# First layer of a diffusion step on one core: first modulation group loaded ahead of x, its copy among the squares, products of constants in TensorE's pauses, first weights converted in parts

## The chip, the cores and the metric

One core of one Trainium2 chip runs the whole program. The metric is device time in microseconds (us) of one execution. TensorE (PE) multiplies, VectorE (DVE), ScalarE (ACT) and GpSimd (POOL) do elementwise work, SyncE (SP) issues most loads. Each engine takes its instructions in a fixed order and waits at the first whose data is missing.

## The reference

Two transformer layers with modulation from a condition vector. Cut to what the change touches, which is the start of layer 0:

```python
def ada_modulation(cond, w_mod, b_mod):
    m = jax.nn.silu(cond) @ w_mod + b_mod
    return jnp.split(m, 6, axis=-1)
...
    sh1_p, sc1_p, ... = ada_modulation(cond_ctx, w_mod[l], b_mod[l])
    sh1_s, sc1_s, ... = ada_modulation(cond_lat, w_mod[l], b_mod[l])
    hp = rms_norm(xp, norm_mix[l]) * (1.0 + sc1_p) + sh1_p    # 128 context tokens
    hs = rms_norm(xs, norm_mix[l]) * (1.0 + sc1_s) + sh1_s    # 512 latent tokens
    p = h @ w_in                                              # both streams, 1024 features in
```

All numbers are float32. Behind it come attention, a feed-forward block and a second layer, which the change does not touch.

## The kernel before

The 640 tokens (512 + 128) lie along the free axis, the 1024 features along the partitions in eight k-tiles of 128. A tile is worked in two halves of 320 tokens (HALF); the second half is split into 192 and 128 where the two streams need different modulation (HCOND), so a step on one k-tile has pieces of 320, 192 and 128 columns.

Float32 accuracy comes from splitting: an operand becomes a rounded high part and a low part, the rest, and a product is three matmuls, high x high, high x low, low x high (mm3). For weights, `unit` loads the raw tile (`load`, into the pool rawp of three buffers), ScalarE copies the high part and VectorE subtracts for the low part. For the activations, Mod.make works on one k-tile and one half: VectorE multiplies x by gain and root (h00t), ScalarE adds the shift and rounds (h00h, the high part), VectorE takes the rest (h00l, the low part).

The stage at the start has these steps, in this order of issue:

- SyncE loads vec, the eight tiles x, and then modulation weights (mraw) and the first three weight tiles (wA0r, wA1r, wA4r).
- Norm.add: ScalarE squares each half of each x (n00sq), VectorE sums them (n00acc). Norm.rstd sums over the partitions by a product with ones on TensorE (n00p); ScalarE takes the logarithm and the exponential of it (n00rs, the root).
- The modulation comes in four groups (mod0, j = 0 to 3), each for two k-tiles. A group's rows are products of the condition (scol) with 2 x 1024 KB of weights, eight instructions for each of two loads; ScalarE copies the result (modsb); two small products with sel turn it into columns, called the turn of the group here; VectorE adds the bias (mods) and makes gains (gs).
- `made(j)` issues the turn of a group and Mod.make of its two k-tiles; `first(ks, us)` issues the weight products of k-tiles ks with weight units us (0, 1 and 2 stand for wA0, wA1 and wA4), twelve matmuls for two halves and two k-tiles in one unit. Their results (wA0a, wA0b, wA1a, wA1b and two banks called wA) collect over all eight k-tiles. Then the products ckv0a begin with the next weights.

The order on TensorE is written out by hand: `run` issues pieces one behind the other, each marked as issued after TensorE's last instruction; `after(inst, fn)` does the same for one instruction of another engine. Where nothing is marked, a scheduler places instructions by its own estimate. The order at the start is:

```python
        nrm.rstd(0)
        run([lambda: nrm.rstd(1)] + rows(0))
        run([lambda: made(0)] + rows(1))
        run([lambda: first((0, 1), [0]), lambda: made(1), lambda: first((0, 1), [1, 2])])
        run(rows(2))
        run([lambda: first((2, 3), [0]), lambda: made(2), lambda: first((2, 3), [1, 2])])
        run(rows(3))
        run([lambda: first((4, 5), [0]), lambda: made(3), lambda: first((4, 5), [1, 2])])
        run([lambda u=u: first((6, 7), [u]) for u in range(3)])
```

## Time and profile before

| what | value |
|---|---|
| median of 3 runs | 1495.97 us (1495.92 to 1497.59) |
| the profiled execution's own time | 1495.85 us |
| its span | 1494.1 us |
| granted TensorE clock, mean | 0.993 |
| TensorE busy | 1445.6 us (97%) |
| VectorE, ScalarE, GpSimd busy | 1210.5, 762.8, 207.3 us |
| start of the products ckv0a | 52.27 us |

The span is the profiled part of an execution; its own time is 1.75 us longer. In rows of the profile, L63 is the helper through which all matmuls go, so they are told apart by tile names. A float32 matmul shows as two records on TensorE, so a count of 32 for a group's rows stands for sixteen instructions. Consecutive rows of one engine overlap a little: the pace is the distance of their starts.

### The profile page before, as it was taken

To read this page: it belongs to the slowest core of one execution; us is meant where nothing else is said; L and a number is where in the kernel's file an instruction comes from. 1 tells how busy PE (TensorE), PEld (TensorE's weight loads), DVE (VectorE), ACT (ScalarE), POOL (GpSimd) and SP (SyncE) were. 2 spreads that over 40 slices of the span, in tenths; PEclk is the share of its full clock that TensorE was granted. 3 is DMA by queue.
4 is the path that set the end of the run, shared out by engine and by line. 5 is a ranking of instruction groups with operands and counts; after the bars stand their busy time and mean duration, and the time that the engine had idled before them with its cause. 6 is when DMAs were issued, how large, how long until landed. Compare 5 with 4: busy or idle time off the path is not lost.

```text
span 1494.1 us, 25710 instructions
## 1 busy us (share of the span) xinstructions
PE 1445.6 (97%) x9785; PEld 1395.6 (93%) x9785; DVE 1210.5 (81%) x2278; ACT 762.8 (51%) x1509; POOL 207.3 (14%) x298
## 2 busy tenths in 40 slices
PE   5999988999999999999999999999999999999996
PEld 4988878889999999999999999989999999999996
DVE  5786687986899999977998878775899999954496
ACT  5445677873755454441123666663755555542242
POOL 0325634432000000000001312222000000000000
PEclk9999999999999999999999999999999999999998
DMA  9544410105155555569764311003155555668522
GB/s 373 215 146 155 150 58 18 43 29 191 50 180 173 187 180 180 181 214 337 272 214 132 114 33 37 33 20 130 49 180 178 181 193 206 211 222 309 194 85 71
DMA packets 79900, 228.59 MB, mean 153 GB/s; under 512 B 8865, under 2 KB 14273, under 8 KB 79393
## 3 DMA queue, kind: packets, MB, share of 16 engines
q1 hardware_dynamic: 76544, 219.40, 42.9%
q0 software_dynamic: 1600, 5.14, 0.9%
q10 hardware_dynamic: 1632, 2.43, 0.5%
q8 instruction: 76, 1.25, 0.3%
q14 instruction: 48, 0.39, 0.1%
HBM read 192.23 MB, written 34.69 MB: 152 GB/s over the span
## 4 chain that ended last, share of the span: by engine, by line
PE 84%; DVE 7%; ACT 5%; issue 2%; DMA 1%; DVEq 0%; ACTq 0%; SPq 0%
PE fg L63 20%; PE fd L63 9%; PE fo L63 8%; PE fu L63 6%; PE gq L63 3%; PE nk L63 2%; PE fo_0b L63 1%; PE fo_2b L63 1%; PE gs L63 1%; PE nq L63 1%; PE fo_2a L63 1%; PE fo_0a L63 1%; PE go L63 1%; PE mod L63 1%; PE ms L63 1%
## 5 line engine op out<-in xcount | busy, mean ns | idle before, releaser
L1759 DVE SCALAR_TENSOR_TENSOR junk<-wm,cb 128x1024 bf16<-128x1024 f32 x62 | 75.7, 1220 | 5.7 <-DMA wm<-in_wm 5.1
L1211 ACT ACTIVATE sg<-g 128x320 f32<-128x320 f32 x34 | 16.0, 472 | 114.9 <-DVE g L1211 114.9
L63 PE MATMUL gq<-h10h,wgq 128*128 128x320 f32 x256 | 66.7, 318 | 0.0
L255 POOL TENSOR_SCALAR h10h<-h10t,gs,mods 128x320 fp32r<-128x320 f32 x4 | 3.6, 891 | 429.5 <-DVE h10t L249 427.8
L1211 DVE SCALAR_TENSOR_TENSOR junk<-wm,cb 128x1024 bf16<-128x1024 f32 x50 | 61.0, 1221 | 0.8
L1211 DVE TENSOR_TENSOR wY<-s,wY 128x1024 fp32r<-128x1024 f32 x40 | 48.8, 1219 | 1.2 <-ACT wY L1211 1.1
L1211 DVE TENSOR_TENSOR wZ<-s,wZ 128x1024 fp32r<-128x1024 f32 x40 | 48.8, 1219 | 0.0
L63 PEld LDWEIGHTS gq<-h10h,wgq 128*128 128x128 f32 x256 | 45.0, 188 | 0.9 <-PE gtp L67 0.2
L1211 ACT ACTIVATE wZ<-s 128x1024 fp32r<-128x1024 f32 x40 | 42.4, 1060 | 0.1
L1211 ACT ACTIVATE wY<-s 128x1024 fp32r<-128x1024 f32 x40 | 42.0, 1049 | 0.0
L1941 ACT ACTIVATE gp<-gs,gb,rq 128x640 f32<-128x640 f32 (+1 forms) x40 | 31.8, 796 | 16.1 <-DVE gb L1940 15.8
L63 PE MATMUL gq<-h10l,wgq 128*128 128x320 f32 x128 | 39.5, 308 | 0.0
L63 PE MATMUL fg<-h11E,wW 128*128 128x320 f32 x240 | 38.7, 310 | 0.0
L63 PE MATMUL fg<-h01q,wX 128*128 128x320 f32 x240 | 38.6, 309 | 0.0
L63 PE MATMUL fg<-h11q,wX 128*128 128x320 f32 x240 | 38.6, 309 | 0.0
L63 PE MATMUL fg<-h11N,wZ 128*128 128x320 f32 x240 | 38.6, 309 | 0.0
L63 PE MATMUL fg<-h01N,wZ 128*128 128x320 f32 x240 | 38.6, 309 | 0.0
L63 PE MATMUL fu<-h11q,wX 128*128 128x320 f32 x240 | 38.6, 309 | 0.0
L63 PE MATMUL fu<-h01q,wX 128*128 128x320 f32 x240 | 38.6, 309 | 0.0
L63 PE MATMUL fg<-h01E,wW 128*128 128x320 f32 x240 | 38.6, 309 | 0.0
L63 PE MATMUL fg<-h11C,wY 128*128 128x320 f32 x240 | 38.5, 309 | 0.0
L63 PE MATMUL fd<-h11q,wZ 128*128 128x320 f32 x240 | 38.5, 309 | 0.0
(3224 smaller groups left out, 5250.6 us busy)
## 6 DMA issues: line engine op xcount, KB each, us to landing
wm<-in_wm SPq DMA_DIRECT2D x48, 512.0 KB, 3.7
mraw<-in_wm SPq DMA_DIRECT2D x8, 1024.0 KB, 15.3
mraw<-in_wm SPq DMA_DIRECT2D x16, 512.0 KB, 3.7
hr_T<-sp_T SPq DMA_DIRECT2D x21, 320.0 KB, 5.8
hr_B<-sp_B SPq DMA_DIRECT2D x18, 320.0 KB, 6.4
mrow<-in_wm0g POOLq DMA_DIRECT2D x8, 512.0 KB, 6.4
wm<-in_wm0g SPq DMA_DIRECT2D x8, 512.0 KB, 3.5
x<-in_xT SPq DMA_DIRECT2D x8, 320.0 KB, 5.3
```

The source lines that it names most:

```text
L63: cls.last = nc.tensor.matmul(*a, **k)
L255: G.tensor_scalar(h[:, c0:c1], t, self.gsl[:, k, 0:1], self.ml[:, self.sh + k, 0:1], ALU.mult, ALU.add)
L1211: self.last = after(self.last, lambda: op(*a, **k))
L1759: def step(kind, at, line=lambda op, *a, **k: op(*a, **k)):
L1941: S.activation(dst, src, AF.Exp, bias=nb, scale=rq[:, j:j + 1], accum_out=ll[:, j:j + 1])
```

## The change

Seven things are moved or cut differently; the arithmetic of the results stays the same.

- The loads of group 0 (mraw0) are issued ahead of x, and wA1r ahead of group 1's.
- The rows of group 0 are issued after the squares of three x, its copy modsb right behind those squares; the other squares are marked as after that copy. Its turn and gains come before the sums n00p.
- Nine products of constants (idle) stand ahead of n00p and five behind; their result is overwritten later.
- The first three weights are converted in a part of 256 columns (two k-tiles) and one of 768; the low part of the 768 columns of wA1 and wA4 goes from VectorE to GpSimd. `after` fixes where the parts stand on ScalarE and VectorE.
- The first h00h waits in ScalarE's order behind a part of wA0 and the second logarithm.
- The first products take k-tiles 0 and 1 in units 0 and 1 before the rows of group 1.
- The rows of groups 1, 2 and 3 and their turns come later in TensorE's order.

```diff
@@ -211,7 +211,7 @@
                 S.activation(self.acc[:, c0:c1], x[:, c0:c1], AF.Square)
             else:
                 sq = tp.tile([P, HT], F32, tag="u", bufs=7, name=f"{self.name}sq{self.k[i]}{i}")
-                S.activation(sq, x[:, c0:c1], AF.Square)
+                self.square = S.activation(sq, x[:, c0:c1], AF.Square)
                 self.last = V.tensor_add(self.acc[:, c0:c1], self.acc[:, c0:c1], sq)
             self.k[i] += 1
 
@@ -220,7 +220,7 @@
             pss = bank(f"{self.name}p{i}")
             PE.matmul(pss[:, :HT], ones, self.acc[:, c0:c1], start=True, stop=True)
             S.activation(self.rs[:, c0:c1], pss[:, :HT], AF.Ln, bias=eps, scale=1.0 / self.n)
-            S.activation(self.rs[:, c0:c1], self.rs[:, c0:c1], AF.Exp, scale=-0.5)
+            self.root = S.activation(self.rs[:, c0:c1], self.rs[:, c0:c1], AF.Exp, scale=-0.5)
             return self.rs
 
     class Mod:
@@ -228,22 +228,22 @@
         def __init__(self, name, x, gsl, ml, sh, even=((0, 2, 4, 6), (0, 2, 5))):
             self.even = even
             self.name, self.x, self.gsl, self.ml, self.sh = name, x, gsl, ml, sh
-            self.act = {}
+            self.act, self.low = {}, {}
             self.hh = [ring.tile([P, T], F32R, tag="hh", name=f"{name}h{k}") for k in range(KT)]
             self.hl = [ring.tile([P, T], F32R, tag="hl", name=f"{name}l{k}") for k in range(KT)]
 
-        def make(self, i, rs, k):
+        def make(self, i, rs, k, at=None):
             h, l = self.hh[k], self.hl[k]
             t = tp.tile([P, HT], F32, tag="u", bufs=7, name=f"{self.name}t{k}{i}")
             o = HALF[i][0]
             if k in self.even[i]:
                 for c0, c1, c in HCOND[i]:
-                    V.scalar_tensor_tensor(t[:, c0 - o:c1 - o], self.x[k][:, c0:c1], self.gsl[:, k, c:c + 1],
-                                           rs[:, c0:c1], ALU.mult, ALU.mult)
+                    after(at, lambda: V.scalar_tensor_tensor(t[:, c0 - o:c1 - o], self.x[k][:, c0:c1], self.gsl[:, k, c:c + 1],
+                                                             rs[:, c0:c1], ALU.mult, ALU.mult))
                 for c0, c1, c in HCOND[i]:
                     b = self.ml[:, self.sh + k, c:c + 1]
                     self.act[k, i] = S.activation(h[:, c0:c1], t[:, c0 - o:c1 - o], AF.Identity, bias=b)
-                    V.scalar_tensor_tensor(l[:, c0:c1], t[:, c0 - o:c1 - o], b, f(h[:, c0:c1]), ALU.add, ALU.subtract)
+                    self.low[k, i] = V.scalar_tensor_tensor(l[:, c0:c1], t[:, c0 - o:c1 - o], b, f(h[:, c0:c1]), ALU.add, ALU.subtract)
                 return
             c0, c1 = HALF[i]
             V.tensor_tensor(t, self.x[k][:, c0:c1], rs[:, c0:c1], ALU.mult)
@@ -333,6 +333,8 @@
     dr0 = l0.enter_context(tc.tile_pool(name="dr0", bufs=1, space=bass.MemoryType.DRAM))
     crs = dr0.tile([2, D], F32, name="crs")
 
+    eased = [None, None]
+
     def mod0(j, bk, load_):
 
         box = []
@@ -351,7 +353,7 @@
                                   stop=half == 1 and g > 1, tile_position=(0, rows.start))
                 if half == 1:
                     box.append(tp.tile([P, HT], F32, tag="u", bufs=7, name=f"modsb{j}"))
-                    S.activation(box[1][:, :256], psm[:, :256], AF.Copy)
+                    eased[0] = after(eased[1], lambda: S.activation(box[1][:, :256], psm[:, :256], AF.Copy))
             return run
 
         def end():
@@ -483,14 +485,21 @@
 
 
     nrm = Norm("n00", D)
+    st = ExitStack()
+    big = st.enter_context(tc.tile_pool(name="start", bufs=1))
+    raws = {}
+
+    def fetch(j):
+        for half in range(2):
+            raws[j, half] = big.tile([P, 2, 1024], F32, tag="mraw", bufs=8, name=f"mraw{j}_{half}")
+            nc.sync.dma_start(raws[j, half], wm0[j, 2 * half:2 * half + 2].rearrange("q p n -> p q n"))
+
+    fetch(0)
     x = []
     for k in range(KT):
         xk = ring.tile([P, T], F32, tag="x", name=f"x0_{k}")
         nc.sync.dma_start(xk, xT[:, k, :])
         x.append(xk)
-    for k in range(KT):
-        for i in range(2):
-            nrm.add(x[k], i)
     hm = Mod("h00", x, gs[0][0], mods[0], SH1, (range(8), range(8)))
     hh, hl = hm.hh, hm.hl
     cnd = keep.tile([P, 2, KT], F32, name="cnd")
@@ -508,42 +517,71 @@
                 for c, (c0, c1) in enumerate(HALF):
                     proj(pss[u][c], *w3[u], hh, hl, [k], c0, c1, first=k == 0, last=k == KT - 1, w0=k)
 
-    with tc.tile_pool(name="start", bufs=1) as big:
-        raws = {}
-
-        def fetch(j):
-            for half in range(2):
-                raws[j, half] = big.tile([P, 2, 1024], F32, tag="mraw", bufs=8, name=f"mraw{j}_{half}")
-                nc.sync.dma_start(raws[j, half], wm0[j, 2 * half:2 * half + 2].rearrange("q p n -> p q n"))
-
-
-        fetch(0)
-        w3 = [unit(wA[0], 1024, "wA0")]
+    with st:
+        wraw = [load(wA[i], 1024, f"wA{i}r") for i in (0, 1)]
         fetch(1)
-        w3 += [unit(wA[i], 1024, f"wA{i}") for i in (1, 4)]
+        wraw.append(load(wA[4], 1024, "wA4r"))
+        w3 = [wp.tile([P, 2, 1024], F32R, tag="w", bufs=3, name=f"wA{i}") for i in (0, 1, 4)]
+        w3 = [(t[:, 0, :], t[:, 1, :]) for t in w3]
+        m = {j: mod0(j, lambda j=j: bank(f"mod{j}", "m"), lambda j, half: [raws[j, half][:, q, :] for q in range(2)]) for j in range(4)}
+        for k in range(KT):
+            if k == 3:
+                eased[1] = nrm.square
+                run(m[0][:2])
+            for i in range(2):
+                after(eased[0] if k > 2 else None, lambda: nrm.add(x[k], i))
+        eased[1] = None
+
+        def convert(u, a, b, act=None, dve=None, eng=V):
+            hi, lw = [t[:, a:b] for t in w3[u]]
+            return (after(act, lambda: S.activation(hi, wraw[u][:, a:b], AF.Copy)),
+                    after(dve, lambda: eng.tensor_tensor(lw, wraw[u][:, a:b], f(hi), ALU.subtract)))
+
         fetch(2)
         fetch(3)
-        m = [mod0(j, lambda j=j: bank(f"mod{j}", "m"), lambda j, half: [raws[j, half][:, q, :] for q in range(2)]) for j in range(4)]
-
-        def made(j):
-
+
+        def gains(j):
             m[j][2]()
             mkgs(0, 0, 2 * j, 2 * j + 2)
+
+        def made(j):
+            if j:
+                gains(j)
             for k in (2 * j, 2 * j + 1):
                 for i in range(2):
-                    hm.make(i, nrm.rs, k)
+                    hm.make(i, nrm.rs, k, hm.low[k - 1, 0] if k == 1 and i == 0 else None)
+
+        def idle(n):
+            for _ in range(n):
+                with tc.issue_after(PE.last.ins):
+                    PE.matmul(pss[2][0][:, :P], ones, ident, start=True, stop=True)
+
+        def begin_h():
+            gains(0)
+            idle(9)
+            nrm.rstd(0)
+            convert(0, 0, 256, nrm.root)
+            after(nrm.root, lambda: nrm.rstd(1))
+            idle(5)
+            hm.make(0, nrm.rs, 0)
+            a, v = convert(1, 0, 256, hm.act[0, 0], hm.low[0, 0])
+            hm.make(1, nrm.rs, 0)
+            hm.make(0, nrm.rs, 1, v)
+            hm.make(1, nrm.rs, 1, v)
+            a, v = convert(0, 256, 1024, hm.act[1, 1], hm.low[1, 1])
+            a, _ = convert(1, 256, 1024, a, eng=G)
+            a, v = convert(2, 0, 256, a, v)
+            convert(2, 256, 1024, a, eng=G)
 
         def rows(j):
             return m[j][:2]
 
-        nrm.rstd(0)
-        run([lambda: nrm.rstd(1)] + rows(0))
-        run([lambda: made(0)] + rows(1))
-        run([lambda: first((0, 1), [0]), lambda: made(1), lambda: first((0, 1), [1, 2])])
-        run(rows(2))
-        run([lambda: first((2, 3), [0]), lambda: made(2), lambda: first((2, 3), [1, 2])])
-        run(rows(3))
-        run([lambda: first((4, 5), [0]), lambda: made(3), lambda: first((4, 5), [1, 2])])
+        begin_h()
+        run([lambda: first((0,), [0, 1]), lambda: first((1,), [0, 1])] + rows(1) + [lambda: made(1), lambda: first((0, 1), [2])])
+        run([lambda: first((2, 3), [0]), lambda: first((2,), [1])] + rows(2) +
+            [lambda: first((3,), [1]), lambda: made(2), lambda: first((2, 3), [2])])
+        run([lambda: first((4, 5), [0])] + rows(3) +
+            [lambda: first((4,), [1]), lambda: made(3), lambda: first((5,), [1]), lambda: first((4, 5), [2])])
         run([lambda u=u: first((6, 7), [u]) for u in range(3)])
     sb = ExitStack()
     ab = sb.enter_context(tc.tile_pool(name="ab", bufs=1, reuse_waits="tile"))
```

TensorE from its first instruction. mod are the rows and the turn of group 0, n00p the sums over the squares, `wA<-ident,ones` the products of constants, wA0a the first weight product. Before:

```order
L67 MATMUL cps<-ident,cnd 16x128
L63 MATMUL n00p_240<-n00acc,ones 128x320
L63 MATMUL n00p_244<-n00acc,ones 128x320
L63 MATMUL mod_248<-mraw_0_209,scol 32x256 x8
L63 MATMUL mod_248<-mraw_1_211,scol 32x256 x8
L63 MATMUL mod_248<-sel,modsb_265 128x4 x2
L63 MATMUL mod_294<-mraw_0_218,scol 32x256 x8
L63 MATMUL mod_294<-mraw_1_220,scol 32x256 x8
L63 MATMUL wA0a<-h00h_177,wA_215 128x320
```

TensorE at the same place now:

```order
L67 MATMUL cps<-ident,cnd 16x128
L63 MATMUL mod_196<-mraw_0_120,scol 32x256 x8
L63 MATMUL mod_196<-mraw_1_122,scol 32x256 x8
L63 MATMUL mod_196<-sel,modsb_213 128x4 x2
L63 MATMUL wA_167<-ident,ones 128x128 x9
L63 MATMUL n00p_267<-n00acc,ones 128x320
L63 MATMUL n00p_273<-n00acc,ones 128x320
L63 MATMUL wA_167<-ident,ones 128x128 x5
L63 MATMUL wA0a<-h00h_140,wA_179 128x320
```

Group 0 moved from behind n00p to ahead of it, and the rows of group 1 (mod_294 before) left the place ahead of the first weight product.

TensorE around the turn of group 2 (k-tiles 4 and 5). The next rows and the first product on k-tile 4 (h00h_181) before; 24 products stand between the turn and those rows, of which the first and the last are shown:

```order
L63 MATMUL wA0b<-h00h_180,wA_215 128x320
L63 MATMUL mod_376<-sel,modsb_393 128x4 x2
L63 MATMUL wA1a<-h00h_179,wA_224 128x320
...
L63 MATMUL wA_205<-h00h_180,wA_229 128x320
L63 MATMUL mod_458<-mraw_0_236,scol 32x256 x8
L63 MATMUL mod_458<-mraw_1_238,scol 32x256 x8
L63 MATMUL wA0a<-h00h_181,wA_215 128x320
```

TensorE at the same turn now, with k-tile 4 as h00h_144 and the first and the last of the 12 products between:

```order
L63 MATMUL wA1b<-h00h_143,wA_180 128x320
L63 MATMUL mod_414<-sel,modsb_431 128x4 x2
L63 MATMUL wA_167<-h00h_142,wA_181 128x320
...
L63 MATMUL wA_168<-h00h_143,wA_181 128x320
L63 MATMUL wA0a<-h00h_144,wA_179 128x320
L63 MATMUL wA0b<-h00h_144,wA_179 128x320
```

Between the turn and the first product on k-tile 4 stood 24 products and the next group's rows; now 12 products stand there, and those rows (mod_490) come after the products of k-tiles 4 and 5 in unit 0.

## The prediction

> **What bounds the kernel now.** I first read the busy time by stage (start:end, length, busy time of each engine with its count, granted clock, DMA share, GB/s).
>
> ```profile
> 0.00:52.27 52.27, 36.51 (x295) 28.66 (x296) 31.52 (x91) 29.51 (x65) 5.71 (x24) 1.00 0.81 305
> 52.27:200.00 147.73, 144.11 (x981) 129.31 (x981) 112.70 (x297) 79.33 (x195) 68.08 (x132) 1.00 0.46 157
> ```
>
> The stage that the change touches ends at 52.27 us, where the products ckv0a begin. TensorE is busy for 36.5 of these 52 us, and nearly always afterwards. The table of TensorE's waits from 130 to 180 us holds two lines only:
>
> ```profile
> PE mod L63 <- ACT modsb L354: 0.2, 1, 0.2
> PE mod L63 <- DMA mraw<-in_wm: 0.2, 1, 0.2
> ```
>
> From 52 to 130 us it has none. The loads there are released by work of the kernel, not by the clock on the wall, so I let every microsecond by which 52.27 moves pass on to the end in full. The question is when ckv0a starts. Next comes TensorE's timeline (start, length, line, output<-inputs, count):
>
> ```profile
> 13.19 2.50 PE L63 MATMUL n00p<-n00acc,ones 128*128 128x320 f32 x4 [7.89 <-DVE n00acc L215]
> 15.62 3.03 PE L63 MATMUL mod<-mraw,scol 128*32 128x256 f32 x32
> 19.16 0.61 PE L63 MATMUL mod<-sel,modsb 128*128 128x4 f32 x4 [0.51 <-ACT modsb L354]
> ...
> 23.88 0.41 PE L63 MATMUL wA0a<-h00h,wA 128*128 128x320 f32 x1
> ...
> 26.23 0.50 PE L63 MATMUL mod<-sel,modsb 128*128 128x4 f32 x4
> ...
> 34.62 0.50 PE L63 MATMUL mod<-sel,modsb 128*128 128x4 f32 x4
> 34.98 0.39 PE L63 MATMUL wA1a<-h00h,wA 128*128 128x320 f32 x1
> ...
> 38.67 1.93 PE L63 MATMUL mod<-mraw,scol 128*32 128x256 f32 x32
> 40.54 0.41 PE L63 MATMUL wA0a<-h00h,wA 128*128 128x320 f32 x1
> ```
>
> The first weight product runs at 23.88, the turn of group 1 (the small products with sel) at 26.23 and that of group 2 at 34.62. A turn holds TensorE for 0.36 us (34.62 to 34.98), the rows of a group for 1.87 (38.67 to 40.54); changing over to them and back costs some 0.2 more, since the product behind each takes 0.1 longer, so I use 0.42 and 2.05. Its pace comes from the chain that ended last (start, length, what, count):
>
> ```profile
> 36.10 0.88 PE wA L63 x6
> ...
> 66.35 1.08 PE cqp L63 x4
> ```
>
> So a weight product takes 0.88 / 6 = 0.147 us at full clock. The two sums of cqp take 1.08 us, those of n00p, of the same size, took 2.50: TensorE ran cold there, at 1.25 us a sum instead of 0.54.
>
> The decisive chain is the making of h00 on VectorE, which follows every turn:
>
> ```profile
> 9.02 4.51 DVE L215 TENSOR_TENSOR n00acc<-n00acc,n00sq 128x320 f32<-128x320 f32 x11
> ...
> 19.86 0.23 DVE L362 TENSOR_TENSOR mods<-mod,vec 128x4 f32<-128x4 f32 x2 [6.14 <-ACT modsb L354]
> 20.13 0.16 DVE L369 SCALAR_TENSOR_TENSOR gs<-mods,vec 128x4 f32<-128x4 f32 x1
> 20.33 0.88 DVE L241 SCALAR_TENSOR_TENSOR h00t<-x,gs,n00rs 128x320 f32<-128x320 f32 x2
> 21.12 1.22 DVE L185 TENSOR_TENSOR wA<-wA0r,wA 128x1024 fp32r<-128x1024 f32 x1
> ...
> 24.63 1.14 DVE L246 SCALAR_TENSOR_TENSOR h00l<-h00t,mods,h00h 128x320 fp32r<-128x320 f32 x3
> ...
> 35.23 0.23 DVE L362 TENSOR_TENSOR mods<-mod,vec 128x4 f32<-128x4 f32 x2 [1.46 <-PE mod L63]
> ...
> 35.69 1.61 DVE L241 SCALAR_TENSOR_TENSOR h00t<-x,gs,n00rs 128x320 f32<-128x320 f32 x4
> 37.21 1.60 DVE L246 SCALAR_TENSOR_TENSOR h00l<-h00t,mods,h00h 128x320 fp32r<-128x320 f32 x4
> 38.73 0.68 DVE L241 SCALAR_TENSOR_TENSOR h00t<-x,gs,n00rs 128x192 f32<-128x192 f32 x2
> 39.67 0.68 DVE L246 SCALAR_TENSOR_TENSOR h00l<-h00t,mods,h00h 128x192 fp32r<-128x192 f32 x2 [0.26 <-ACT h00h L245]
> ```
>
> From the turn at 34.62 to the last h00l of that pair at 40.35 pass 5.73 us. Before, TensorE has 24 products (3.5 us) and the rows of the next group (2.05 us) to do meanwhile, so it never sees this.
>
> **The change, step by step.** *x behind the first modulation weights.* Two transfers of 1024 KB now stand ahead of x. When x0 and wA1r were issued (SyncE's queue), what the DMA engines moved (GB/s, last column), and when the two landed (us from their issues):
>
> ```profile
> 1.18 4.58 SPq L489 DMA_DIRECT2D x<-in_xT  x8
> ...
> 9.69 0.34 SPq L164 DMA_DIRECT2D wA1r<-in_wA  x1
> ```
>
> ```profile
> 0.00:5.00 5.00, 0.08 (x1) 0.09 (x1) 0.64 (x6) 2.01 (x4) 0.70 (x6) 1.00 0.60 187
> 5.00:10.00 5.00, 0.30 (x1) 0.00 (x0) 2.83 (x10) 4.93 (x12) 0.00 (x0) 1.00 1.00 353
> ```
>
> ```profile
> x<-in_xT SPq DMA_DIRECT2D x1, 320.0 KB, 3.3
> ...
> wA1r<-in_wA SPq DMA_DIRECT2D x1, 512.0 KB, 14.4
> ```
>
> That is 0.94 MB by 5 us and 2.70 MB by 10. The table vec, the four kr and mraw0 (about 2.24 MB) are through at 8.7 us, x0 about 0.9 later. With larger packets it could come at 8.8, with the other transfers between them at 10.6; I take 9.7, against 1.18 + 3.3 = 4.5 before.
>
> *Squares, with group 0 among them.* ScalarE's rows:
>
> ```profile
> 6.62 5.62 ACT L214 ACTIVATE n00sq<-x 128x320 f32<-128x320 f32 x14
> 14.66 0.53 ACT L222 ACTIVATE n00rs<-n00p,eps 128x320 f32<-128x320 f32 x1 [2.42 <-PE n00p L63]
> 15.22 0.47 ACT L223 ACTIVATE n00rs<-n00rs 128x320 f32<-128x320 f32 x1
> ...
> 40.73 0.38 ACT L354 ACTIVATE modsb<-mod 128x256 f32<-128x256 f32 x1 [0.81 <-PE mod L63]
> ```
>
> Six squares at 0.40 (2.4), the copy modsb (0.4), from the turn to mods 0.7 (19.16 to 19.86), mods and gs (0.4): while VectorE waits for these, the sums behind them in its queue wait too. Then nine sums at 0.41 up to the first half of x7: 3.8. So n00p can start 7.7 us after x0, at 17.4, against 13.19. The rows of group 0 (3.03 us) and the turn no longer follow it. The nine products of constants run from about 13.0; cold, at most 1.25 x 128/320 = 0.5 us each, they end at 17.5, so they cost nothing or 0.1; without this cover n00p would run cold. It takes 0.7 to 1.47 us until ScalarE starts (before: 13.19 to 14.66); I take 1.1. With 1.06 for the logarithm and the root, h00t starts at 19.55, against 20.33. The five products of constants behind n00p fill a wait of TensorE for h00h and cost nothing either.
>
> *First weights in two parts.* VectorE does 2 x 0.34 us instead of 1.14 in the first making, but ScalarE puts a part of wA0 and the second logarithm ahead of the first h00h: 0.5 us. The first making (before: 20.33 to 25.77, 5.44) then takes 5.5, to 25.1; six products that need its last piece follow: 26.0. wA1r lands sooner, mraw1 behind it, with about the bytes ahead of it that wA1r had before, so near 9.69 + 14.4 = 24.1: the rows of group 1 find their data at 26.0. tabK, wA2r and wA3r take over the room of the first three weights, some 3 us later than now; they are used beyond 49 us, so that is hidden.
>
> *Rows of groups 1 to 3 later.* Here lies the loss. Group 1: rows 2.05, modsb and the way to it 0.5, with the turn right behind on TensorE: the turn is at 28.6, against 26.23. Behind each turn now stand only 12 products (1.76 us), then those on the new h00. From a turn to the end of these: 5.73 (the rows above) + 0.3 for the last two products = 6.0, where TensorE has 0.42 + 1.76 + 1.76 = 3.9 to do: 2.1 us of waiting. For group 1 VectorE puts 0.34 of wA4 into the chain: 6.4. Then:
>
> - turn 1 to turn 2: 6.4 + 6 products 0.88 + rows 2.05 + 6 products 0.88 = 10.2: 38.8
> - turn 2 to turn 3: 6.0 + 2.05 + 0.88 = 8.95: 47.75 (18 products cover turn 3)
> - turn 3 to ckv0a: 6.0 + 24 products 3.53 = 9.55: 57.3
>
> *GpSimd does 768 columns of wA1 and wA4.* The first lies beside a wait of VectorE; the second beside the making of group 1. Its price alone, and what VectorE's steps cost beside GpSimd's sums of two tensors (66 to 76 us) and without:
>
> ```profile
> L185 POOL TENSOR_TENSOR oaw<-oaw1r,oaw 128x1024 fp32r<-128x1024 f32 x1 | 2.4, 2379 | 1.9 <-ACT oaw L184 1.9
> L569 DVE SCALAR_TENSOR_TENSOR cqr<-cqr,vec,cqrs 128x320 f32<-128x320 f32 x4 | 2.7, 732 | 0.0
> L752 POOL TENSOR_TENSOR bm<-gt,msk 128x128 f32<-128x128 f32 x6 | 5.0, 861 | 8.0 <-DMA gt<-in_rpbp 8.0
> L246 DVE SCALAR_TENSOR_TENSOR h00l<-h00t,mods,h00h 128x320 fp32r<-128x320 f32 x8 | 4.4, 550 | 0.0
> ```
>
> At 0.75 x 2.38 = 1.8 us and a third more for VectorE's steps (732 against 550), that is +0.6 within turn 1's chain; the bounds are 0 and 1.0. The Trainium skill (GPSIMD Engine Reference, 8. Key points) says that GpSimd shares its SBUF interfaces with VectorE and that VectorE instructions with two SBUF inputs contend with it, as h00t and h00l have; the L569 row agrees. By its table in 4.1 the part would take about twice VectorE's time, an estimate of 1.8 us (1.22 x 0.75 x 2), which leaves the sum as it is.
>
> **Sum.** 57.3 + 0.6 - 52.27 = +5.6 us. The profiled execution took 1495.85 us at a span of 1494.1; with +5.6 it is 1501.45, and its own time is 0.1 under the median of the runs, 1495.97. I forecast 1501.5: slower, through h00 that TensorE now waits for after every turn. A difference within 0.2% (3 us) can't be told from no change.
>
> **Rivals.**
>
> *Not slower: the waits after the turns are shorter than the chain says.* Without them TensorE's own work from turn 1 at 28.6 is 120 products (17.6), two groups of rows (4.1) and three turns (1.3): ckv0a at 51.6, or 1495.2. The waits sum to 5.7 us in my forecast; up to 3.6 of them the kernel stays within 0.2% of before, and none of them with x0 at 8.8 and a warm n00p gives 1493.9; only if the making also came 1.0 us sooner would it be faster by over 0.2%. For it: idle products and products earlier in the order keep TensorE going. Against it: ScalarE and VectorE do the same instructions after a turn, and 34.62 to 40.35 is measured, with no wait over 0.26 us in it.
>
> *The clock falls back in the waits.* TensorE's work in 20 to 35 us is broken up. If one stretch of 3 us ran at n00p's pace (0.62 per 320 columns against 0.27), it loses 1.7 us: 1503.2. Against it: before, the pieces between 19 and 23 us were broken up too, and the rows there ran at full pace.
>
> *x comes sooner.* With x0 at 8.8, a warm n00p and no contention, -0.9 - 0.4 - 0.6: 1499.6, still slower, since turn 1 also needs mraw1 (24.1, then half the rows and the copy: 25.6) and 28.7 us follow it: 54.3 at the best, +2.0.
>
> **How the numbers follow.** Forecast, with its terms at both ends (1499.6 to 1503.0): 0.72. Clock falls back: 0.10. Waits partly gone, within 0.2%: 0.13. Faster: 0.05. So slower 0.82, same 0.13, faster 0.05. The bounds: x0 -0.9/+0.9, n00p -0.4/+0.4, contention -0.6/+0.4, fall-back +1.7. Of the rival within 0.2%, the part above 1498.3 I take in; below lie about 0.1, above 1503.8 about 0.07.
>
> **What would show it.** Right: mraw0 lands near 9 us, x0 near 10; n00p starts near 17.4; the first wA0a at about 21 (h00t at 19.55, then h00h behind the logarithm), nearly 3 us sooner; turns near 28.6, 39 and 48; TensorE waits for DVE h00l and ACT h00h in wA0a and wA0b by 2 us a group; ckv0a near 58; from there on the shift stays. Wrong: turns 8 us apart, or a shift at 52 us that is given back by 200 us.

## The result, and the profile after

The changed kernel takes 1506.37 us (median of four runs, 1503.62 to 1506.72) against 1496.24 us for the kernel before on the same chip: 1.0063 times as long, 95% interval 1.0051 to 1.0075. In two later rounds it took 1503.13 to 1506.29 (five runs, ratio 1.0052, interval 1.0038 to 1.0065) and 1502.96 to 1506.58 (three single runs). The median of all twelve is 1505.6. I had forecast 1501.5, with 1503.8 as the upper end: slower for the reason given, but by 10.1 us and not by 5.6.

The profiled run took 1506.49 us at a span of 1504.7. By stage (start:end, length, busy time of PE, PEld, DVE, ACT and POOL with counts, granted clock, DMA share, GB/s), the start of the kernel now reaches to 61 us:

```profile
0.00:61.00 61.00, 46.52 (x322) 35.70 (x323) 31.37 (x92) 29.38 (x68) 9.35 (x26) 0.97 0.69 260
61.00:200.00 139.00, 138.40 (x953) 125.45 (x952) 105.44 (x273) 72.50 (x179) 67.01 (x129) 1.00 0.48 165
```

TensorE's timeline of the changed kernel shows the sums n00p, the four turns and the rows between them (start, length, what, count, wait ahead of it):

```profile
13.43 1.01 PE L63 MATMUL mod<-sel,modsb 128*128 128x4 f32 x4 [1.67 <-ACT modsb L356]
14.30 4.19 PE L63 MATMUL wA<-ident,ones 128*128 128x128 f32 x18
18.51 2.14 PE L63 MATMUL n00p<-n00acc,ones 128*128 128x320 f32 x4
...
27.55 1.93 PE L63 MATMUL mod<-mraw,scol 128*32 128x256 f32 x32
29.99 0.61 PE L63 MATMUL mod<-sel,modsb 128*128 128x4 f32 x4 [0.50 <-ACT modsb L356]
...
33.19 0.70 PE L63 MATMUL wA<-h00h,wA 128*128 128x320 f32 x3 [1.90 <-DVE wA L538]
...
42.17 0.50 PE L63 MATMUL mod<-sel,modsb 128*128 128x4 f32 x4
...
51.29 0.50 PE L63 MATMUL mod<-sel,modsb 128*128 128x4 f32 x4
```

Turn 1 is at 29.99 (before 26.23), turn 2 at 42.17 (34.62), turn 3 at 51.29 (42.40 in the same view of before). The first product of ckv0a stands at 60.99 in this view, before at 52.11: 8.9 us later. (The prediction's 52.27 is the chain's row of it.) The wait of 1.90 us is new. VectorE's and GpSimd's timelines show what stood behind it:

```profile
31.12 0.23 DVE L364 TENSOR_TENSOR mods<-mod,vec 128x4 f32<-128x4 f32 x2 [3.51 <-ACT wA L537]
31.27 1.86 DVE L538 TENSOR_TENSOR wA<-wA4r,wA 128x256 fp32r<-128x256 f32 x1
33.06 0.15 DVE L371 SCALAR_TENSOR_TENSOR gs<-mods,vec 128x4 f32<-128x4 f32 x1
33.24 1.61 DVE L241 SCALAR_TENSOR_TENSOR h00t<-x,gs,n00rs 128x320 f32<-128x320 f32 x4
```

```profile
31.05 1.80 POOL L538 TENSOR_TENSOR wA<-wA4r,wA 128x768 fp32r<-128x768 f32 x1 [1.75 <-ACT wA L537]
```

The subtraction of 128x256 takes 1.86 us beside GpSimd's sum; the same one for wA0 took 0.42 at 21.51. The making of group 1 starts that much later.

The waits of TensorE between 21 and 61 us (total, times, longest), where before had 1.4 us for mraw1 and 0.3 us behind turn 1:

```profile
PE wA0b L63 <- ACT h00h L245: 2.1, 4, 0.8
PE wA L63 <- DVE wA L538: 1.9, 1, 1.9
PE mod L63 <- ACT modsb L356: 0.5, 1, 0.5
PE wA0a L63 <- ACT h00h L245: 0.5, 1, 0.5
PE wA0a L63 <- DVE h00l L246: 0.2, 1, 0.2
```

This lists only 5.2 us. The rest of the loss is in products that run slower or start late one by one while h00 is made, which is why I compare turns, not waits.

### The profile page after: what moved, and what is told of

Its sections match the earlier page's. It is cut to its first block, busy times and chain, and to the rows that moved or that the text cites. A ratio compares the mean times of both kernels' runs of the same rounds, so it can differ in the third digit from the quotient of the medians.

```text
span 1504.7 us, 25779 instructions
## 1 busy us (share of the span) xinstructions
PE 1458.1 (97%) x9813; PEld 1404.8 (93%) x9813; DVE 1210.2 (80%) x2279; ACT 762.8 (51%) x1512; POOL 211.9 (14%) x300
## 4 chain that ended last, share of the span: by engine, by line
PE 82%; DVE 9%; ACT 5%; issue 2%; DMA 1%; SPq 0%; DVEq 0%; ACTq 0%
PE fg L63 19%; PE fd L63 9%; PE fo L63 7%; PE fu L63 5%; PE gq L63 3%; PE nk L63 2%; PE nq L63 2%; PE fo_2b L63 1%; PE fo_0b L63 1%; PE gs L63 1%; PE fo_2a L63 1%; PE fo_0a L63 1%; PE go L63 1%; PE mod L63 1%; PE ms L63 1%
## 5 line engine op out<-in xcount | busy, mean ns | idle before, releaser
L63 PE MATMUL fd<-h01q,wZ 128*128 128x320 f32 x240 | 38.6, 309 | 1.2 <-ACT p L1249 1.2
```

The costliest lines, as they stand in the source:

```text
L63: cls.last = nc.tensor.matmul(*a, **k)
```

## The experiments

Read from the timelines of all profiled runs: the starts of turn 1 and ckv0a (its first product), the stretches between, and what is left of the span behind ckv0a (us).

| run | turn 1 | 1 to 2 | 2 to 3 | 3 to ckv0a | ckv0a | behind it | span |
|---|---|---|---|---|---|---|---|
| before | 26.23 | 8.39 | 7.78 | 9.71 | 52.11 | 1442.0 | 1494.1 |
| h0, before again | 28.57 | 7.78 | 7.78 | 9.71 | 53.84 | 1441.5 | 1495.3 |
| changed | 29.99 | 12.18 | 9.12 | 9.70 | 60.99 | 1443.7 | 1504.7 |
| c0, changed again | 30.24 | 12.19 | 9.12 | 9.70 | 61.25 | 1443.2 | 1504.5 |
| h1 | 30.15 | 12.17 | 9.12 | 9.70 | 61.14 | 1443.7 | 1504.8 |
| h2 | 29.31 | 12.18 | 9.12 | 9.70 | 60.31 | 1443.6 | 1503.9 |
| h3 | 30.33 | 12.18 | 9.12 | 9.70 | 61.33 | 1439.9 | 1501.2 |
| c1, rows ahead | 30.03 | 9.56 | 7.78 | 9.71 | 57.08 | 1439.8 | 1496.9 |
| c2, wA4 later | 28.84 | 10.74 | 9.12 | 9.70 | 58.40 | 1442.1 | 1500.5 |
| f1, both | 30.35 | 8.22 | 7.78 | 9.71 | 56.06 | 1439.9 | 1496.0 |
| c3, x first | 32.70 | 10.26 | 9.13 | 9.70 | 61.79 | 1443.7 | 1505.5 |
| f2, mraw1 sooner | 31.00 | 7.88 | 7.78 | 9.71 | 56.37 | 1444.2 | 1500.6 |
| f3, before shifted | 33.41 | 7.78 | 7.78 | 9.70 | 58.67 | 1442.2 | 1500.9 |
| g1, no constants | 30.59 | 10.10 | 9.12 | 9.69 | 59.50 | 1441.3 | 1500.8 |
| g2, more constants | 28.85 | 12.72 | 9.12 | 9.70 | 60.39 | 1440.9 | 1501.3 |
| g3, mraw0 alone | 29.16 | 9.32 | 7.78 | 9.70 | 55.96 | 1441.9 | 1497.9 |
| f4, before, two parts | 27.75 | 7.79 | 7.78 | 9.71 | 53.03 | 1442.2 | 1495.2 |
| g4, the same, mended | 27.13 | 7.78 | 7.78 | 9.70 | 52.39 | 1441.2 | 1493.6 |
| i1, before, filled | 26.02 | 8.28 | 7.78 | 9.70 | 51.78 | 1442.5 | 1494.3 |
| i2, g4 filled | 26.30 | 8.21 | 7.78 | 9.70 | 51.99 | 1440.2 | 1492.2 |

In the five profiled runs of the changed kernel the stretches between turns repeat to 0.02 us; turn 1 and the stretch behind ckv0a don't. In the kernel before, turn 1 to turn 2 took 8.39 us in one run and, with a later turn 1, 7.78 in the other.

**c0: the changed kernel again.**

> The changed kernel once more, as the yardstick for the others beside it. All theories: 1506.4 us, ckv0a at 61.0 and 1.7 us more lost between 430 and 445 us, where ScalarE waits for the transfer of hd_0h. If that later loss is chance, some of the runs lie near 1503.6, as one of four did.

1503.94 us (1503.13 to 1506.29). The times fall into two groups, near 1503.5 and near 1506; h0 to h3 below say what divides them.

**c1: the rows of groups 2 and 3 ahead again.**

```diff
-        run([lambda: first((0,), [0, 1]), lambda: first((1,), [0, 1])] + rows(1) + [lambda: made(1), lambda: first((0, 1), [2])])
-        run([lambda: first((2, 3), [0]), lambda: first((2,), [1])] + rows(2) + ...
+        run([lambda: first((0, 1), [0])] + rows(1) + [lambda: made(1), lambda: first((0, 1), [1, 2])])
+        run(rows(2))
+        run([lambda: first((2, 3), [0]), lambda: made(2), lambda: first((2, 3), [1, 2])])
...
```

> The changed kernel, but with the rows of groups 2 and 3 ahead of the products that cover them and all of units 1 and 2 behind each turn, as before the change. Theory 1, the waits behind the turns are most of the loss: turn 1 at 28.7, from it to ckv0a 132 products (19.4), two groups of rows (4.1) and three turns (1.3), with up to 1.5 us for wA4: ckv0a at 53.5 to 55.5 and 1499 to 1501 us. Theory 2, GpSimd's sum on wA4 and the late start are most of it: ckv0a goes back by less than 2 us, 1504.5 or more.

1499.96 us (1498.64 to 1503.06, ratio 1.0025, interval 1.0016 to 1.0034). ckv0a comes 4.2 us sooner than in c0 (57.08), short of theory 1's 53.5 to 55.5, since turn 1 stays at 30.03 and TensorE still waits 1.4 us for wA4. From turn 2 to turn 3 it is 7.78, as before. The edit also puts the products of unit 1 back behind the turns, so what it weighs is the whole order of rows, turns and products. That order is a large part of the loss and not all of it. VectorE and GpSimd behind turn 1 of c1:

```profile
31.43 1.50 DVE L371 SCALAR_TENSOR_TENSOR gs<-mods,vec 128x4 f32<-128x4 f32 x1
32.86 0.41 DVE L538 TENSOR_TENSOR wA<-wA4r,wA 128x256 fp32r<-128x256 f32 x1
```

```profile
31.09 1.82 POOL L538 TENSOR_TENSOR wA<-wA4r,wA 128x768 fp32r<-128x768 f32 x1 [2.67 <-ACT wA L537]
```

Here gs comes first, 128x4 numbers that take 0.15 us elsewhere, and it takes 1.50, to the end of GpSimd's sum at 32.91; the 128x256 behind it takes 0.41. It isn't a slowdown by a third: by these ends VectorE stands still until GpSimd is through.

**c2: the later part of wA4 behind the making, without GpSimd.**

```diff
-            convert(2, 256, 1024, a, eng=G)
...
+            if j == 1:
+                convert(2, 256, 1024, hm.act[3, 1], hm.low[3, 1])
```

> The changed kernel, but columns 256 to 1023 of wA4 are copied by ScalarE and subtracted by VectorE only behind the making of group 1, where both are idle; GpSimd has no part of wA4. Theory 2 (GpSimd's sum stalls VectorE, and mods waits for ScalarE's copy): the part of 128x256 on VectorE takes 0.42 us instead of 1.86, mods comes 0.5 us sooner, turn 1 to turn 2 takes 10.3 instead of 12.2, so 1504.5 us. Theory 1 alone (TensorE's waits have the length of the order's making): turn 1 to turn 2 shrinks by less than 0.5, 1506 us.

1503.45 us (1502.30 to 1504.98), beside c0's 1503.94. In the profile the mechanism is clear:

```profile
30.12 0.42 DVE L538 TENSOR_TENSOR wA<-wA4r,wA 128x256 fp32r<-128x256 f32 x1
30.46 0.15 DVE L371 SCALAR_TENSOR_TENSOR gs<-mods,vec 128x4 f32<-128x4 f32 x1
30.65 1.61 DVE L241 SCALAR_TENSOR_TENSOR h00t<-x,gs,n00rs 128x320 f32<-128x320 f32 x4
```

0.42 us instead of 1.86, and turn 1 to turn 2 takes 10.74 instead of 12.19: 1.45 us. The other half of what I had expected fell: mods still comes 1.13 us behind the start of turn 1, as in c0, so ScalarE's copy of the later columns had not held it, though c0's profile names ScalarE. (Where wA4's first part is already done, in g1, it is 0.71; I did not find out why.) The changed kernel also has a fall of the granted clock in this stretch, which c2 does not have (below). It takes no part in the 1.45 us: from the row of the last h00l (37.22 in the changed kernel's profile, 34.62 in c2) to turn 2 it is 4.95 us in one and 4.96 in the other. The gain in the times is too small against their spread to be seen there.

**f1: both edits at once.**

> The changed kernel with both edits at once: rows and turns as before the change, and wA4's columns 256 to 1023 left to ScalarE and VectorE behind the making of group 1. If the wait for wA4 in c1 (1.4 us) was all that stood between turn 1 and turn 2 beside the order, turn 1 to turn 2 takes 8.2 to 8.4 (before: 8.39) instead of 9.56, and ckv0a follows turn 1 by 26 us (before: 26.04): at 55.0 to 56.0, by when turn 1 comes (28.8 to 30.0), 1498 to 1499.5 us. If another wait takes its place, 9.5 stays and so does 1500 us.

1498.24 us (1496.74 to 1501.19, ratio 1.0017, interval 1.0008 to 1.0025). Turn 1 to ckv0a takes 25.71 us, as expected, and before 25.88. The one wait of TensorE from 30 to 56 us is this:

```profile
PE mod L63 <- ACT modsb L356: 0.5, 1, 0.5
```

So these two account for what is lost behind turn 1, to within 0.5 us (h0 and f3, before's order with a later turn 1, take 25.27): in c0 31.01, in f1 25.71, 5.3 us. With GpSimd's sum out of the way the order of rows and turns is worth 10.74 + 9.12 - 8.22 - 7.78 = 3.9 us, GpSimd's sum 1.45. What is left of f1's distance, 4.0 us at ckv0a, is the late turn 1.

**f3: does a delay pass on?**

```diff
+        run([lambda: idle(35), lambda: first((0, 1), [0]), lambda: made(1), ...
```

> The kernel before, with 35 products of constants on TensorE right ahead of its first weight product (0.256 us each at full clock: 9.0 us); nothing else is changed. It tells whether a plain delay of TensorE passes on to the end. If in full, ckv0a comes 8 to 9 us later and the end later by the same within 0.3. If what lies behind ckv0a depends on when it starts, the stretch from ckv0a to the end differs from before's by 1 to 2 us, as it did in the changed kernel (1443.7 against 1441.8).

```profile
23.74 8.08 PE L63 MATMUL wA<-ident,ones 128*128 128x128 f32 x70
```

ckv0a came 6.56 us later (58.67) and not 8 to 9, since some of the 8.08 us covered waits; the span grew by 6.8: the delay passes on in full. The times grew by 7.3 (1503.39 against 1496.14).

**c3, g3, f2: what makes turn 1 late.** In c3 x stands first again, and the rows of group 0 behind all squares; g3 is the kernel before with mraw0 ahead of x and nothing else; f2 is f1 with mraw1 ahead of wA1r.

```diff
 c3, in the changed kernel             f2, in f1
-    fetch(0)                          -  wraw = [load(wA[i], ...) for i in (0, 1)]
     x = [] ... loads of x             +  wraw = [load(wA[0], ...)]
+    fetch(0)                             fetch(1)
```

> The changed kernel, but x stands ahead of the first modulation weights again, and the rows of group 0 and their copy behind all squares. Theory 3 (the late x and the cold n00p cost 1.5 us that the earlier rows don't give back): x0 at 4.5, n00p near 17, h00t at 19.4 instead of 21.05, turn 1 at 28.5 instead of 30.0, 1504.9 us. Rival: turn 1 is set by the landing of mraw1, whose bytes ahead are the same; then turn 1 moves by less than 0.5 and the time is 1506 us.

> The kernel before with one part of the change alone: the loads of group 0's modulation weights stand ahead of x. Theory (late x is paid in full where nothing is gained by the earlier rows): x0 at 10 instead of 4.5, n00p near 17.5 instead of 13.2, the rows of group 0 behind it now without a wait, h00t at 22.5 to 23.2 instead of 20.33, ckv0a 2.2 to 2.9 us later, 1498.5 to 1499. Rival: turn 1 waits for mraw1 in both, and less than 1 us is left of it, 1497.

> As the kernel with both edits, and the load of group 1's modulation weights stands ahead of wA1r in SyncE's queue again. Theory: turn 1 is late because 512 KB more stand ahead of mraw1 (1.3 us at 400 GB/s), so the rows of group 1 end at 28.2 instead of 29.5, turn 1 at 28.7, ckv0a at 54.7, 1498 us. Rival: turn 1 is set by the late x (first making ends at 25.5 to 26.4 whatever the loads), then it comes no more than 0.3 us sooner.

c3 missed: 1507.56 us (1504.21 to 1508.89), since its rows of group 0 stand ahead of n00p in TensorE's queue and their data now lands at 14.5 to 17; n00p starts at 21.95, h00t at 23.75. It shows that the two moves belong together. g3 took 1498.50 (1497.34 to 1501.18, ratio 1.0017, interval 1.0008 to 1.0026): n00p at 16.98 instead of 13.19, h00t at 23.27 instead of 20.33, turn 1 at 29.16 and ckv0a at 55.96; 0.9 us of that arose behind turn 1, where its clock fell for 3.4 us. The late x alone costs before's order 2.9 us at h00t; in the changed kernel, whose turn 0 lies ahead of n00p, h00t stands at 19.75 to 21.05. f2 missed too, 1501.76 (1499.23 to 1502.39): wA1r came late instead, and h00h waited for its copy.

```profile
25.55 0.41 PE L63 MATMUL wA0a<-h00h,wA 128*128 128x320 f32 x1 [1.20 <-ACT h00h L245]
...
27.77 2.71 PE L63 MATMUL mod<-mraw,scol 128*32 128x256 f32 x32
```

But these rows took 2.71 us, in c1 3.07, where others take 1.93. That is the clock. Stretches of c0, of h0 (the kernel before), of the changed kernel and of c2, one row each; the granted clock is the third number from the end:

```profile
24.00:27.00 3.00, 3.00 (x13) 3.00 (x13) 2.19 (x5) 2.16 (x4) 0.75 (x1) 0.51 1.02 407
```

```profile
24.00:27.00 3.00, 2.99 (x20) 1.72 (x21) 1.86 (x6) 2.28 (x5) 0.00 (x0) 0.50 1.03 411
```

```profile
30.00:37.00 7.00, 5.10 (x24) 4.80 (x25) 5.80 (x14) 2.90 (x7) 1.80 (x1) 0.77 1.03 404
```

```profile
30.00:37.00 7.00, 5.76 (x35) 4.13 (x38) 5.97 (x17) 3.13 (x7) 0.00 (x0) 1.00 0.94 370
```

By single microseconds, the clock of c0 is at 0.50 for 3.4 us from 24.1 on, ahead of turn 1, and again for 3.4 us behind it. Of the five profiled runs of the changed kernel, c0, h1 and h3 have it ahead of turn 1, and all five behind it. In h0 it fell for 6.8 us, and turn 1 of the kernel before came at 28.57 instead of 26.23; the second load of its rows also landed 1.1 us later (24.01 against 22.88), so the clock has about half of that. TensorE then does 0.27 us a product instead of 0.147: from h00t to the rows of group 1 it takes 7.96 us in c0, h1 and h3 and 6.50 in the other two, 1.5 us less. The fall behind turn 1 costs nothing (12.17 to 12.19 wherever it lies), because TensorE waits for h00 there anyway; only in g2, where it lasted 6.8 us, is it 12.72. The Trainium skill (TensorE: Matmul & The Clock Gate, Part 1) has a half-rate clock that follows TensorE's activity in free-running windows of 3.4 us; the lengths 3.4 and 6.8 agree with it. Its table under "Why this matters for your kernels" avoids such drops by leaving no idle gaps over about 3 us. That would not have been enough here: the longest wait in the 10 us ahead of c0's fall is 0.8 us.

**g1 and g2: the products of constants.** g1 has none of the fourteen, g2 has seven more (three ahead of the rows of group 0, four behind them).

> The changed kernel without its fourteen products of constants. As the prediction has it, n00p runs cold without this cover: 1.25 us for each sum, 1.47 us until ScalarE starts, so h00t comes 0.4 us later than with a warm n00p (c0: 1.34 us for both sums) and 0 to 0.1 us later than in the profiled run of the changed kernel, where it was cold anyway. Rival: with nothing ahead of it n00p starts as soon as its sums are there and h00t is not later at all. The first weight products then run cold too.

> The changed kernel with seven more products of constants, three ahead of the rows of group 0 and four behind them, so that TensorE has hardly a hole from 5 us on. If the nine products came too late to bring the clock up (4.2 us at 0.465 each), these bring it up sooner: n00p takes 1.1 us for both sums from its start near 18.0, and the products just ahead of it 0.26 instead of 0.465 each; h00t 0.5 to 0.7 us sooner than in the profiled run of the changed kernel against the landing of x0. Rival: the clock comes up by the wall or not at all: 0.465 stays.

TensorE in g1, then in g2:

```profile
17.86 2.50 PE L63 MATMUL n00p<-n00acc,ones 128*128 128x320 f32 x4 [4.07 <-DVE n00acc L215]
```

```profile
11.07 2.08 PE L63 MATMUL wA<-ident,ones 128*128 128x128 f32 x8
...
13.76 4.04 PE L63 MATMUL wA<-ident,ones 128*128 128x128 f32 x18
18.00 1.34 PE L63 MATMUL n00p<-n00acc,ones 128*128 128x320 f32 x4 [0.20 <-DVE n00acc L215]
```

Without them n00p takes 2.50 us, cold throughout; with nine it takes 1.34 to 2.14 in the five profiled runs, and seven more don't help: 0.45 to 0.52 us a product as far as 17.8, though TensorE hardly stood still from 5 us on. So the cover is worth 0.2 to 0.6 us at h00t, counted from x0 (10.43 us in g1, 9.80 to 10.23 in the five), and the rival in the expectation for g2 holds. The cover is worth more behind h00t: without it the first weight products of g1 take 0.27 us each as far as 26.4, and its rows of group 1 start at 28.15 instead of 26.41 in g2, neither with the granted clock below 1.00 there. g1 (1502.78, one run; g2 took 1503.07) also shows where GpSimd's part costs nothing: there its sum and wA4's subtraction met at 27 us, when nothing waited for them, and turn 1 to turn 2 took 10.10.

**h0 to h3: the later stretch.**

> The kernel before, once more under the profile. If what lies behind ckv0a varies by chance from run to run, its stretch from ckv0a to the end differs from 1441.8 us by up to 2 us here too; if it is fixed, it is 1441.8 within 0.3.

> The changed kernel. If the later wait is chance, the run has either the wait for the transfer of hd_0h near 436 us and about 1506 us, or not and about 1503.8. If it belongs to the change, it is there in every look.

> As the look before it: 1506 with the wait for the transfer of hd_0h, or 1503.8 without, if the wait is chance.

> As the looks before it: 1506 with the wait for the transfer of hd_0h, or 1503.8 without, if the wait is chance.

They took 1497.07, 1506.58, 1505.64 and 1502.96. h3 starts ckv0a as late as the others (61.33) and is 3.3 to 3.8 us shorter behind it. ScalarE at 437 us in the changed kernel's profile and the transfer that it waits for (KB, us from issue to landing), then the same two of h3:

```profile
437.49 0.74 ACT L1291 ACTIVATE hd_0h<-sg 128x640 fp32r<-128x640 f32 x1 [3.56 <-DMA sp_0h<-hd_0h]
```

```profile
sp_0h<-hd_0h SPq DMA_DIRECT2D x1, 320.0 KB, 6.7
```

```profile
434.30 0.74 ACT L1291 ACTIVATE hd_0h<-sg 128x640 fp32r<-128x640 f32 x1 [0.60 <-DVE sg L1307]
```

```profile
sp_0h<-hd_0h SPq DMA_DIRECT2D x1, 320.0 KB, 3.3
```

Where this transfer takes 6.5 to 6.7 us, ScalarE and then TensorE wait (TensorE 1.0 to 1.2 us), and the kernel loses some 1.6 us against h3; where it takes 3.2 to 5.5, TensorE does not wait. Some 1.5 us more of h3's lead arose between 820 and 983 us, and the rest before 425; I did not look for their causes. Only h3 among the profiled runs belongs to the lower group of times, so that such waits divide the two groups is likely and not shown. This loss was in four of five profiled runs of the changed kernel and in c3 and f2, in neither of the kernel before (5.1 and 5.3 us) and in none of c1, c2, f1, f3. ckv0a alone doesn't set it (c2 and f3 start it at 58.4 and 58.7, f2 at 56.4), so whether it belongs to the change stays open.

**f4, g4, i1, i2: is there a better kernel?** f4 keeps of the change only the first weights in two parts, all on VectorE, with before's loads and order. In g4 the first part of wA1 stands behind group 0's making. i1 is the kernel before, and i2 is g4, with seven products of constants in the two waits ahead of turn 1.

```diff
 i1
-        run([lambda: made(0)] + rows(1))
+        run([lambda: made(0), lambda: idle(2), rows(1)[0], lambda: idle(5), rows(1)[1]])
```

> The loads, the squares and the order of TensorE as before the change; kept of the change are the first weights in two parts (columns 0 to 255 first), with all subtractions on VectorE and the later parts of wA1 and wA4 behind the making of group 1. Theory: with x and mraw0 in before's order and the rows ahead, the two parts are worth what they take out of VectorE's queue, 0.8 us in the first making and up to 2 us ahead of group 1's, of which TensorE felt about 1: ckv0a at 51 to 52, 1494.5 to 1496. Rival: the making of group 0 waits for turn 0 anyway, and nothing changes: 52.3, 1496.3.

> As the kernel with before's order and the first weights in two parts, but the first part of wA1, for which VectorE's queue waited 1.04 us in the midst of group 0's making, stands behind that making. Theory: the first making ends at 25.5 or sooner, turn 1 at 26.0, ckv0a 25.3 later at 51.3, 1495.3 us, 1 us under before and too little to tell by the times alone. Rival: another load is late in its place (wA0r, mraw0 or mraw1), turn 1 stays at 27 or later and ckv0a at 52.3 to 53.

> The kernel before with seven products of constants in the waits ahead of turn 1: two behind turn 0, five between the two halves of the rows of group 1. If the waits there make the granted clock fall, it stays at 1.00 from 15 to 35 us, turn 1 comes at 26.2 and ckv0a at 52.1 in this look, and the median of the times is up to 1 us under before's, whose looks stood at 52.1 and 53.8. Rival: the clock falls by chance whatever TensorE does; then 0.50 shows as often, and the time is before's.

> As g4 (before's order, first weights in two parts), with the same seven products of constants. g4 had the clock at 0.50 from 22.3 to 25.6 us and turn 1 at 27.13. With the clock at 1.00 the second half of the rows takes 1.07 instead of 1.93, the products behind them 0.15 instead of 0.27 each: turn 1 at 25.9 to 26.2, ckv0a 25.26 later at 51.2 to 51.5, 1495 us, the best of all kernels here by 0.7 to 1 us, which is at the edge of what the times can tell. Rival: the clock falls all the same, 52.4 and 1496.8.

f4 took 1497.68 (ratio 1.0012, interval 1.0003 to 1.0021): wA1's part waited 1.04 us for its data in VectorE's queue, and the clock fell for 3.4 us at 22.5. g4 took 1496.77 (1.0005, 0.9996 to 1.0014) without that wait and with the same fall. The second half of g4's rows ran at half clock; in i1 and i2 it doesn't (g4 first, then i1, then i2):

```profile
22.92 1.93 PE L63 MATMUL mod<-mraw,scol 128*32 128x256 f32 x16 [1.49 <-DMA mraw<-in_wm]
```

```profile
21.59 1.38 PE L63 MATMUL wA<-ident,ones 128*128 128x128 f32 x10
23.15 1.07 PE L63 MATMUL mod<-mraw,scol 128*32 128x256 f32 x16 [0.17 <-DMA mraw<-in_wm]
```

```profile
21.72 1.38 PE L63 MATMUL wA<-ident,ones 128*128 128x128 f32 x10
23.06 1.07 PE L63 MATMUL mod<-mraw,scol 128*32 128x256 f32 x16
```

Both have the clock at 1.00 throughout from 15 to 36 us, and turn 1 at 26.02 and 26.30. i1 takes 1494.69 us (1493.76 to 1497.26, ratio 0.9988, interval 0.9979 to 0.9997), i2 1494.35 (1493.96 to 1496.46, 0.9991, 0.9982 to 1.0000). The two can't be told apart; i1 is the smaller change and alone has an interval below 1, so seven products and nothing else beat the kernel before by 0.03 to 0.21%. That this gain is the clock is not shown: i1's profiled run starts ckv0a 0.33 us sooner than before's and is 0.2 us longer in its span. Of the profiled runs in before's order without the products, the clock fell ahead of turn 1 in three (h0, f4, g4) and not in three (before, f3, g3); two runs with them can't show that they prevent it.

## Why the prediction was wrong in its size

The loss is where the prediction put it, and ckv0a's shift reaches the end as it said (f3). Term by term:

- **x and n00p**: x0 at 9.94 to 10.14 in c0 and h1 to h3 and 10.82 in the first profiled run, forecast 9.7 (to 10.6). n00p follows x0 by 7.7 to 7.9, forecast 7.7; "without this cover n00p would run cold" is so (g1), but with it n00p ran cold in the first run too (1.47 us until ScalarE starts, the upper bound). h00t at 21.05 there and at 19.75 to 20.37 in the other four, forecast 19.55.
- **Turn 1 at 28.6**: 29.3 to 30.3 in five runs. The making (5.38 us against 5.5) and the way from the rows to the turn (2.44 against 2.6) were right. What failed differs by run. In three of five it is TensorE's pace ahead of them, where the clock fell: 1.5 us. In the other two h00t was late: 0.8 us in h2, and 1.5 in the first profiled run, of which 1.1 are x0's later landing and 0.4 the cold n00p. The rival "the clock falls back" had 0.10 and 1.7 us; its price was near, its chance far too low, and the argument against it, that before's pieces at 19 to 23 us were broken up without a fall, rested on one profile: in h0 they fell.
- **From a turn to the end of the making**: 6.0 and 6.4 were near. Without GpSimd turn 1 to turn 2 takes 10.74 (c2) where I had 10.2, most of it mods, which came 1.13 us behind the turn and 0.6 behind the other turns; turn 2 to turn 3 9.12 (8.95), turn 3 to ckv0a 9.70 (9.55). The three sum to 29.56, 0.9 us above the forecast.
- **GpSimd's part of wA4 at +0.6, with 1.0 as the bound**: it costs 1.45. This step failed in its kind. I took the slowdown of VectorE beside other sums of GpSimd (732 against 550 ns) as a rate, where here VectorE waits for GpSimd's whole instruction, and I counted only the making's steps, where the subtraction ahead of them caught it. The four steps behind the 732 ns did not run slower either: each ended 0.34 to 0.35 us behind one of a row of GpSimd's sums, so they took turns with them.
- **Everything passes on, and nothing more**: passes on, yes, but the first profiled run is 1.7 us longer behind ckv0a, while h3 is 2.1 us shorter there than before's profile. I had no term for that.

For the first profiled run, 5.6 + 1.4 (turn 1) + 0.9 (the three stretches) + 0.9 (GpSimd) + 1.7 (behind ckv0a) = 10.5, of its 10.6 us of span. The rival "the waits are shorter" fell: they are longer.

## What to carry to other kernels

Before moving work behind a dependent step, count from the profile how much TensorE has left to do during the chain that the step starts; the rows, turns and products moved by one step cost 3.9 us here. An engine that helps out costs what the other engine has to do in that time, so place its part where the other has nothing due (g1 and c2 against c0). Where TensorE waits ahead of a dependent step, watch the granted clock too: a fall of 3.4 us cost 1.5 us here. Filling the waits with products of constants is cheap to try (i1), though two runs don't show that it holds the clock.

## What the runs showed of the hardware that I had not expected

- A VectorE instruction with two inputs from SBUF that starts while GpSimd's sum of two tensors is under way ends 0.02 to 0.35 us after that sum whatever its size: 128x256 in 1.86 us (0.42 alone), 128x4 in 1.50 us (0.15 alone), while mods, which reads the products' accumulators, took its usual 0.23 beside it. The kernel before had such rows already. A sum of 128x320 there, 0.49 us elsewhere, and GpSimd's instruction beside it, which ends at 373.03:

```profile
370.84 2.54 DVE L215 TENSOR_TENSOR oanacc<-oanacc,oansq 128x320 f32<-128x320 f32 x1
```

```profile
370.52 2.51 POOL L185 TENSOR_TENSOR oaw<-oaw7r,oaw 128x1024 fp32r<-128x1024 f32 x1 [1.30 <-ACT oaw L184]
```

The Trainium skill (GPSIMD Engine Reference, 8. Key points) has the shared interfaces and the two SBUF inputs as the condition, which these rows agree with; the size, the whole rest of GpSimd's instruction, is read from the rows. Where VectorE starts first, it is GpSimd that is held: a sum of 128x320 of its own at 821.10 us in the kernel before took 2.02 us, where 0.9 to 1.0 is usual.
- The granted clock fell to 0.50 for 3.4 us, or twice that, in or behind waits of 0.5 to 1.9 us, in some runs of a kernel and not in others. That the waits caused it is not shown. At the start, when products took 0.465 us instead of 0.256, the same column read 1.00.
- The same 320 KB transfer took 3.3 to 6.7 us to land in profiled runs of the same kernel; the long ones go with some 1.6 us at the end.
